# Another order of the seven products of w_co, with the sums made head by head and the second half's rows normalised first

## The chip, the cores and the metric

The kernel runs on one core of a Trainium2 chip. The metric is the device time of one execution in microseconds (us). The engines are TensorE (PE, with its weight loads as PEld), VectorE (DVE), ScalarE (ACT), GpSimd (POOL) and SyncE (SP), which issues the DMAs. Each engine works through its own queue in order.

## What is computed

One layer of an encoder trunk on x of 1024 tokens x 1024, in float32: a mixer (windowed attention and a gated DeltaNet), a cross-attention into 256 memory tokens, and a SwiGLU FFN. Each part is followed by an RMS norm, and its result is added to the residual stream. The change touches the cross-attention's output projection, what is around it, and the order of the rows from there on.

```python
def _memory_cross_attention(h, mem_n, w_q, w_kv, w_o):
    q = (h @ w_q).reshape(b, s, CROSS_HEADS, CROSS_HEAD_DIM)
    ...
    p = jax.nn.softmax(jnp.einsum('bqhd,bkhd->bhqk', q, k) * (CROSS_HEAD_DIM ** -0.5), axis=-1)
    o = jnp.einsum('bhqk,bkhd->bqhd', p, v).reshape(b, s, D_MODEL)
    return o @ w_o
...
    c = _memory_cross_attention(_rms_norm(x, g_cross_pre[l]), _rms_norm(mem, g_mem[l]), w_cq[l], w_ckv[l], w_co[l])
    x = x + _rms_norm(c, g_cross_post[l])
    f = _swiglu(_rms_norm(x, g_ffn_pre[l]), w_gate_up[l], w_down[l])
    x = x + _rms_norm(f, g_ffn_post[l])
```

## The kernel before

**Precision.** Every matmul operand is split into a high part (ACT casts it to fp32r, L103) and a low part (DVE or POOL subtracts the high part from the source, L104). A product takes three matmuls: high with high, high with low, low with high. `load_w` fetches weights over SP into `wraw` and splits them into `whi` and `wlo`.

**Stages.** The mixer comes first, then w_out by halves of 512 tokens (`mid_gemm`), then the cross-attention by halves (`cross_q`, `cross_attention`), w_co, the FFN's gate and up products, and w_down. Gate/up, w_co and w_down are computed with seven block products in place of eight: both operands are cut into 2 x 2 blocks, and sums of blocks take part in the products.

**Attention of a half.** For each of 4 heads: scores `pcs` (PE, L1158), maximum and its scaling `cmx` (DVE, L1160 and L1161), exponentials `cpr` (ACT, L1165), reciprocal `csum` and multiplication of `cpr` (DVE, L1167 and L1168), transposes `pct` (PE, L1174), their split into `cph` and `cpl`, and the value product `pco` (PE, L1184) of two column tiles ct = 2h and 2h + 1, each [128 columns x 512 tokens] and already transposed as w_co needs it.

**The blocks of the activations.** The first half's outputs are A11 (ct 0 to 3) and A12 (ct 4 to 7). They are copied to `raw` (`oraw`, L1188) and split in place into the query operand `q0`. The second half's are A21 and A22. For ct below 4 ACT copies A21 to `s1_` (tile `os1`, L1193), DVE subtracts it from A11 into `cs3` (L1195, a buffer of the tag `wpart`), and S3 = A11 - A21 is split into `q1`. For ct from 4 on A22 is split into `q1`, and DVE makes three sums in place: S1 = A21 + A22 in `s1_` (L1199), S2 = S1 - A11 in the first half of `raw` (L1200), S4 = A12 - S2 in its second half (L1201).

**The blocks of the weights.** w_co's four blocks b11, b12, b21, b22 are loaded over SP (8 transfers, tile `wco`) while the second half's attention runs, and POOL makes T1, T3, T2 and T4 from them in place by 16 differences (L1266; `sums` and `later`, called from the first two products).

**The seven products**, each 4 k tiles x 4 blocks of 128 tokens x 3 = 48 matmuls (L1245), in this order (names as in the prediction):

| | operands | banks | then |
|---|---|---|---|
| P1 | A11, B11 (both straight from `q0` and w_co) | A | ACT copies it to `e_` (L1319, tile `p1`) |
| P2 | A12, B21 | A, on top | ACT copies C11 to `c11` (L1323) |
| P3 | S3 (split in `q1`), T3 = `b12` | Y | DVE: `zv` = `e_` + Y |
| P4 | S2, T2 = `b22` | X | DVE: `e_` += X, `za` = `zv` + X |
| P5 | S1, T1 = `b11` | Z | DVE: `za` += Z |
| P6 | S4, B22 from w_co | Z, on top | DVE: `zz` high half = `e_` + Z |
| P7 | A22 (split in `q1`), T4 = `b21` | X, on top | DVE: `zv` += X |

P1 to P6 run k tile by k tile over all four token blocks (`block_product`); P7 runs block by block of tokens, so that its rows end one after the other. S2, S1 and S4 are split just before they are used, all three into one pair of tiles, `part` (`act_part`). Blocks of weights are split k tile by k tile into the tag `wpart` (`weight_part`, 7 buffers; a k tile takes two).

**The tail.** `zz` holds the first half's rows 0 to 3 (in blocks of 128 tokens), `zl` (`zv` and `za`) the rows 4 to 7. `square_of` (ACT, L1270) sums squares, `gained` (DVE or POOL, L1312) multiplies by the gain. `finish` takes one block of rows: it loads the residual `xr` over SP (L1279), makes the root on POOL (`prs`, L1281 and L1282), adds on DVE (L1283), stores x2 over SP (L1284), sums squares again on ACT (L1286), makes a second root on POOL (`pr`, L161 and L162) and normalises on ACT (L1290) or DVE (L1292). Rows 0 to 3 finish under P7 with the last step on ACT, rows 4 to 7 after it with the last step on DVE. Rows 0 and 1 have their own residual tile `xr01`, all others share two buffers `xr`. Then PE transposes the rows (`ptn`, L1367): the first four blocks of rows become X11 and X21, whose low parts POOL makes, and the last four go into X22 and the sums T1 to T4 of the FFN. The first FFN products (`pA`, L1412, EARLY = 4 pairs of gate and up) need the first four blocks of rows alone.

**Who sets the order.** The source gives the program order; a scheduler then places every instruction on its engine's queue by priority and by its own timeline. Weight loads and splits (`load_w`, `weight_part`, `act_part`) have a priority raised by AHEAD = 300, so they move ahead as far as their buffers allow.

Of the kernel before, what the change touches and what calls it, by code (L numbers as in the profile page):

```python
# [76 lines left out]
def tile_hybrid_block(  # L77
# [1057 lines left out]
    s1_ = rg.tile([P, KT // 2, HALF], F32, tag="os1", name="os1")  # L1135
# [10 lines left out]
    def cross_attention(q, hf):  # L1146
        for h in range(4):
# [31 lines left out]
            for j in range(2):  # L1179
# [11 lines left out]
                k = ct % (KT // 2)  # L1191
                if ct < KT // 2:
                    nc.scalar.copy(s1_[:, k], po)  # L1193
                    d_ = rg.tile([P, HALF], F32, tag="wpart", name="cs3", bufs=7)
                    nc.vector.tensor_tensor(d_, raw[:, k], po, ALU.subtract)  # L1195
                    split(q[0][:, k], q[1][:, k], d_)
                    continue
                split(q[0][:, ct, :], q[1][:, ct, :], po)
                nc.vector.tensor_tensor(s1_[:, k], s1_[:, k], po, ALU.add)  # L1199
                nc.vector.tensor_tensor(raw[:, k], s1_[:, k], raw[:, k], ALU.subtract)  # L1200
                nc.vector.tensor_tensor(raw[:, ct], raw[:, ct], raw[:, k], ALU.subtract)  # L1201
# [16 lines left out]
    zz = opC.tile([P, 4, D], F32, tag="x22", name="zz")  # L1218
# [3 lines left out]
    zl = tz.tile([P, 4, D], F32, name="zl")  # L1222
# [6 lines left out]
    def weight_part(b_, k):  # L1229
        with tc.high_priority(AHEAD):  # L1230
            dh, dl = (rg.tile([P, HALF], F32R, tag="wpart", name="wpart", bufs=7) for _ in range(2))
            split(dh, dl, b_[:, k])
        return dh, dl

    def act_part(a, k0):
        if isinstance(a, tuple):
            return [h[:, k0:k0 + 2] for h in a]
        with tc.high_priority(AHEAD):
            ah, al = (t[:, k0:k0 + 2] for t in part)
            split(ah, al, a[:, k0:k0 + 2])  # L1240
# [31 lines left out]
    def finish(r, z, eng):  # L1272

        tok = slice(r * P, (r + 1) * P)
        if r < 2:
            xr = xr01[:, r]
# [18 lines left out]
    s2_, s4_ = blocks(raw)  # L1295
# [28 lines left out]
    part = [p_.tile([P, HK, HALF], F32R, tag=t_, name="part") for p_, t_ in ((opB, b0 + "1"), (opB3, "b31"))]  # L1324
    Y = four([PG] * 4)
    block_product(Y, s3_, b12)
    for t in range(4):
        add(zv[:, t], e_[:, t], Y[t])
        square_of(c11[:, t], 0, t)
        gained(zz[:, t, LO], c11[:, t], LO)  # L1330
    X = four([PX] * 2 + [PN] * 2)
    block_product(X, s2_, b22, last=False)
    for t in range(4):
        add(e_[:, t], e_[:, t], X[t])
        add(za[:, t], zv[:, t], X[t])
    xr01 = opB3.tile([P, 2, D], F32, tag="b30", name="xr01")
    Z = four([PG] * 4)
    block_product(Z, s1_, b11, last=False)
    for t in range(4):
        add(za[:, t], za[:, t], Z[t])  # L1340
        square_of(za[:, t], 1, 4 + t)
        gained(za[:, t], za[:, t], HI)
    block_product(Z, s4_, (1, 1), first=False)
    for t in range(4):
        add(zz[:, t, HI], e_[:, t], Z[t])
        square_of(zz[:, t, HI], 1, t)
        gained(zz[:, t, HI], zz[:, t, HI], HI, nc.vector)
        finish(t, zz[:, t], nc.scalar)
    acts = [act_part(a22, k0) for k0 in (0, 2)]
    wts = [weight_part(b21, k) for k in range(HK)]  # L1350
    for t in range(4):
        for k in range(HK):
            ah, al = (h[:, k % 2] for h in acts[k // 2])
            three(X[t], ah, al, *wts[k], slice(t * P, (t + 1) * P), False, k == HK - 1, False)
        add(zv[:, t], zv[:, t], X[t])
        square_of(zv[:, t], 0, 4 + t)
        gained(zv[:, t], zv[:, t], LO, nc.vector)
        finish(4 + t, zl[:, t], nc.vector)
# [11 lines left out]
    def first_rows(j, k):  # L1370
        return zz[:, j, k * P:(k + 1) * P]

    def last_rows(j, k):
        return zl[:, j, k * P:(k + 1) * P]

    for k in range(KT):
        pt = turned_k(first_rows, k)
        nc.scalar.activation(raw[:, k, :], pt, AF.Identity, scale=gain("ffn", k))
        split(x1h[:, k, :], x1l[:, k, :], raw[:, k, :], eng=nc.gpsimd)
# [243 lines left out]

    def residual(t, after=None):
        xr = tp_.tile([P, D], F32, tag="xrf", name="xrf")
        with tc.issue_after((after or late).ins):
            nc.sync.dma_start(xr, d_x2[t * P:(t + 1) * P, :])
# [37 lines left out]
    def first_half(t):  # L1665
# [5 lines left out]
        nc.sync.dma_start(out[t * P:(t + 1) * P, :], z)  # L1671
# [14 lines left out]
    for t in range(4):  # L1686
# [20 lines left out]
        for z, o_ in ((za, 512), (zv, 0)):  # L1707
            nc.vector.scalar_tensor_tensor(z[:, t], z[:, t], rs, xr[:, o_:o_ + 512], ALU.mult, ALU.add)
            nc.sync.dma_start(out[r * P:(r + 1) * P, o_:o_ + 512], z[:, t])
# [32 lines left out]
```

## Time and profile before

| | us |
|---|---|
| median of 3 runs (lowest, highest) | 1556.82 (1551.7, 1563.44) |
| profiled execution, its time | 1557.34 |
| profiled execution, its span | 1555.6 |

The page of the profile covers one execution from its first to its last instruction (the span). Each row of instructions names the line, the engine, the operation and the tiles; in brackets at the end stands the idle time of the engine before it and what ended that. `pst` is the PSUM tile of all seven products. Mean granted PE clock over the span: 0.985 of full speed.

### The profile page before, as it was taken

Reading aid. Unit: us, or ns where it says so; the run is one execution under the profiler, and the core shown is the slowest. Engines: PE = TensorE matmul, PEld = TensorE weight load, DVE = VectorE, ACT = ScalarE, POOL = GpSimd, SP = SyncE. Lnnn points to the kernel's source line nnn. Section 1 sums busy time; section 2 is a strip of 40 time slices with the busy share of each in tenths; the row PEclk is TensorE's granted clock in tenths of the full one; section 3 lists DMA queues with packets and bytes.
Section 4 is the critical chain, followed back from the end, with each engine's and each line's share of the span. In section 5 each row is a group of like instructions: output and inputs, shape, how many; then the busy total and the mean of one; then the engine's idle time right before and its main releaser. Section 6 shows DMA issues by size and latency. Waiting matters only on the chain. (4 is left out here: it accounts for less than half of the span.)

```text
span 1555.6 us, 21081 instructions
## 1 busy us (share of the span) xinstructions
PE 1484.2 (95%) x7403; PEld 1243.1 (80%) x7403; DVE 1104.5 (71%) x1752; ACT 749.9 (48%) x1526; POOL 441.9 (28%) x436
## 2 busy tenths in 40 slices
PE   6999999998899899999998788999999999999998
PEld 5888888877899788888886567888888888888786
DVE  6868999776888865545388666776868554696665
ACT  6579722357567754545364564332323332454532
POOL 2020222302336103442251653433534333000021
PEclk9999999999999999999999799999999999999999
DMA  6244585847986764521422345344434333863355
GB/s 204 75 121 132 159 201 147 215 143 226 333 257 204 246 229 154 183 88 55 161 70 68 117 146 159 103 133 129 140 116 131 102 102 102 295 226 102 108 174 164
DMA packets 264167, 241.91 MB, mean 156 GB/s; under 512 B 33768, under 2 KB 203645, under 8 KB 264061
## 3 DMA queue, kind: packets, MB, share of 16 engines
q1 hardware_dynamic: 264061, 240.57, 49.5%
q8 instruction: 58, 0.95, 0.3%
q14 instruction: 48, 0.39, 0.1%
HBM read 171.02 MB, written 66.88 MB: 153 GB/s over the span
## 5 line engine op out<-in xcount | busy, mean ns | idle before, releaser
L103 ACT CAST whi<-wraw 128x1024 fp32r<-128x1024 f32 x98 | 103.1, 1053 | 156.2 <-issue 41.4
L104 POOL TENSOR_TENSOR wlo<-wraw,whi 128x1024 fp32r<-128x1024 f32 x38 | 91.8, 2415 | 184.3 <-ACT whi L103 182.8
L261 PE MATMUL pg<-hlo,whi 128*128 128x512 f32 x352 | 139.4, 396 | 0.0
L261 PE MATMUL pg<-hhi,whi 128*128 128x512 f32 x352 | 139.3, 396 | 0.0
L261 PE MATMUL pg<-hhi,wlo 128*128 128x512 f32 x352 | 138.5, 394 | 0.0
L1412 PE MATMUL pA<-b,whi 128*128 128x512 f32 x352 | 112.6, 398 | 6.5 <-POOL b L104 2.9
L104 DVE TENSOR_TENSOR wlo<-wraw,whi 128x1024 fp32r<-128x1024 f32 x60 | 79.2, 1322 | 46.7 <-ACT whi L103 44.1
L1412 PEld LDWEIGHTS pA<-b,whi 128*128 128x128 f32 x352 | 66.3, 191 | 22.2 <-POOL b L104 4.5
L1603 PE MATMUL pdX<-dhl,whi 128*128 128x512 f32 x264 | 76.1, 390 | 1.5 <-ACT dhl L103 0.8
L261 PEld LDWEIGHTS pg<-hhi,whi 128*128 128x128 f32 x352 | 66.4, 189 | 13.3 <-ACT hhi L103 0.2
L261 PEld LDWEIGHTS pg<-hhi,wlo 128*128 128x128 f32 x352 | 66.5, 189 | 12.8
L261 PEld LDWEIGHTS pg<-hlo,whi 128*128 128x128 f32 x352 | 66.3, 188 | 12.8
L1490 POOL TENSOR_TENSOR act<-act,up 128x512 f32<-128x512 f32 x33 | 49.8, 1509 | 91.5 <-DVE up L1489 60.5
L1412 PE MATMUL pA<-b,wlo 128*128 128x512 f32 x176 | 69.2, 395 | 0.2 <-DVE wlo L104 0.2
L103 ACT CAST whi<-araw 128x1024 fp32r<-128x1024 f32 (+1 forms) x36 | 35.4, 983 | 67.3 <-PE pdX L1603 24.5
L1633 POOL TENSOR_SCALAR frs<-sq 128x1 f32<-128x1 f32 x8 | 12.0, 1498 | 194.0 <-ACT jk L1622 193.1
L104 DVE TENSOR_TENSOR wlo<-araw,whi 128x1024 fp32r<-128x1024 f32 (+1 forms) x36 | 40.9, 1136 | 35.5 <-ACT whi L103 35.3
L286 DVE SCALAR_TENSOR_TENSOR acc<-cp,cols,acc 128x1024 f32<-128x1024 f32 x48 | 62.2, 1298 | 0.1
L1603 PEld LDWEIGHTS pdX<-dhl,whi 128*128 128x128 f32 x264 | 49.3, 188 | 12.8 <-ACT dhl L103 1.1
L1462 POOL TENSOR_TENSOR sr<-wraw 128x512 f32<-128x512 f32 x22 | 29.5, 1342 | 100.0 <-DMA wraw<-in_w_gate_up_dram 100.0
L1463 DVE TENSOR_TENSOR sr<-sr,wraw 128x512 f32<-128x512 f32 x22 | 36.7, 1667 | 28.1 <-POOL sr L1462 28.1
L1412 PE MATMUL pB<-s,s1h 128*128 128x512 f32 x176 | 54.3, 390 | 2.0 <-ACT s1h L103 2.0
(472 smaller groups left out, 4340.0 us busy)
## 6 DMA issues: line engine op xcount, KB each, us to landing
wraw<-in_w_gate_up_dram SPq DMA_DIRECT2D x52, 512.0 KB, 3.9
kv<-d_kv SPq DMA_DIRECT2D x32, 512.0 KB, 6.8
wraw<-in_w_in_dram SPq DMA_DIRECT2D x22, 512.0 KB, 4.6
b<-in_w_down_dram SPq DMA_DIRECT2D x20, 512.0 KB, 7.8
araw<-d_as SPq DMA_DIRECT2D x20, 512.0 KB, 3.7
pz<-d_pz SPq DMA_DIRECT2D x32, 256.0 KB, 6.6
wraw<-in_w_ckv_dram SPq DMA_DIRECT2D x16, 512.0 KB, 6.0
wraw<-in_w_out_dram SPq DMA_DIRECT2D x16, 512.0 KB, 3.7
```

Source lines behind the costliest of these rows:

```text
L103: nc.scalar.copy(hi, src)
L104: (eng or nc.vector).tensor_tensor(lo, src, f32(hi), ALU.subtract)
L261: nc.tensor.matmul(p_, w[:, k, :], ah[a][:, k, :], start=(k == 0 and i == 0), stop=(k == nk - 1 and i == 2))
L286: nc.vector.scalar_tensor_tensor(acc, cp[:, t:t + S], taps[t], acc, ALU.mult, ALU.add)
L1412: nc.tensor.matmul(out_, w[a][:, k, :], xx[b_][:, k, :], start=(start and k == 0 and i == 0), stop=(k == HK - 1 and i == 2), skip_group_ch ...
L1462: nc.gpsimd.tensor_tensor(s[0], b_[:, 0:HK], b_[:, HK:], ALU.add)
L1463: nc.vector.tensor_tensor(s[1], s[0], a_[:, 0:HK], ALU.subtract)
L1490: nc.gpsimd.tensor_tensor(o_, o_, up, ALU.mult)
L1603: nc.tensor.matmul(banks[t], a[:, k - k0, tt], w, start=(first and k == 0 and i == 0), stop=(k == NB - 1 and i == 2), skip_group_check=not ...
L1633: nc.gpsimd.tensor_scalar(rs, sq[:, 1, t:t + 1], sq[:, 0, t:t + 1], D * EPS, ALU.add, ALU.add)
```

## The change

The cross-attention's second half keeps no copy of A21. For ct from 4 on, S2 is made at once as (A22 - high part of S3) - low part of S3 (two DVE operations), split by ACT and DVE into `part` inside the attention's loop, and used to update `raw`: S1 = A11 + S2 in its first half, S4 = A12 - S2 in its second. The differences of the second half go into a tile `cs` of the attention's pool, and `wpart` has 9 buffers.

The order of the products becomes P1, P2, P3, P7, P4, P5, P6. P7 runs on top of P3 in the banks Y, after DVE has written P1 + P3 into `y7`, which is the memory of `b12`; so the sums after the products are four more operations. P4 takes S2 from `part`. The splits of S1 and S4 go into the memory of `q1` that P7 and P3 have read. P6 now runs by token blocks, with its weights loaded ahead from w_co.

Rows 4 to 7 are finished first, under P6, rows 0 to 3 after it, in both cases with the last step in turn on ACT and DVE. `zl` and `zz` change their pools, `xr45` takes the place of `xr01`. The FFN takes rows 4 to 7 as its first half; half of the low parts of X11 and X21 go to DVE. `there` puts the rows back when w_down reads the residual and stores the output.

```diff
--- before.py
+++ after.py
@@ -1132,7 +1132,6 @@
     raw = LR2.enter_context(pool("raw2", 1, side="right")).tile([P, KT, HALF], F32, name="oraw")
     LG = ExitStack()
     rg = LG.enter_context(pool("rg", 1, side="right"))
-    s1_ = rg.tile([P, KT // 2, HALF], F32, tag="os1", name="os1")
 
     def cross_q(hf):
         q = operand(opB, ("s1", "s2")[hf])
@@ -1188,17 +1187,26 @@
                     nc.scalar.copy(raw[:, ct], po)
                     split(q[0][:, ct, :], q[1][:, ct, :], po)
                     continue
-                k = ct % (KT // 2)
-                if ct < KT // 2:
-                    nc.scalar.copy(s1_[:, k], po)
-                    d_ = rg.tile([P, HALF], F32, tag="wpart", name="cs3", bufs=7)
+                k = ct % HK
+                if ct < HK:
+                    d_ = tx.tile([P, HALF], F32, tag="cs", name="cs")
                     nc.vector.tensor_tensor(d_, raw[:, k], po, ALU.subtract)
                     split(q[0][:, k], q[1][:, k], d_)
                     continue
                 split(q[0][:, ct, :], q[1][:, ct, :], po)
-                nc.vector.tensor_tensor(s1_[:, k], s1_[:, k], po, ALU.add)
-                nc.vector.tensor_tensor(raw[:, k], s1_[:, k], raw[:, k], ALU.subtract)
-                nc.vector.tensor_tensor(raw[:, ct], raw[:, ct], raw[:, k], ALU.subtract)
+                d_ = tx.tile([P, HALF], F32, tag="cs", name="cs")
+                nc.vector.tensor_tensor(d_, po, f32(q[0][:, k]), ALU.subtract)
+                nc.vector.tensor_tensor(d_, d_, f32(q[1][:, k]), ALU.subtract)
+                split(*(t[:, k] for t in s2_part()), d_)
+                nc.vector.tensor_tensor(raw[:, k], raw[:, k], d_, ALU.add)
+                nc.vector.tensor_tensor(raw[:, ct], raw[:, ct], d_, ALU.subtract)
+
+    part = []
+
+    def s2_part():
+        if not part:
+            part.extend(p_.tile([P, HK, HALF], F32R, tag=t_, name="part") for p_, t_ in ((opB, b0 + "1"), (opB3, "b31")))
+        return part
 
     q0 = cross_q(0)
     cross_attention(q0, 0)
@@ -1215,11 +1223,11 @@
 
 
     opC = LX.enter_context(pool("opC", 1))
-    zz = opC.tile([P, 4, D], F32, tag="x22", name="zz")
+    zl = opC.tile([P, 4, D], F32, tag="x22", name="zl")
     L3 = ExitStack()
     tz = L3.enter_context(pool("tz2", 1))
     gp = gpost_tile(tz, g_cross_post)
-    zl = tz.tile([P, 4, D], F32, name="zl")
+    zz = tz.tile([P, 4, D], F32, name="zz")
     zv, za = zl[:, :, 0:HALF], zl[:, :, HALF:]
     ssq = tz.tile([P, 2, NT], F32, name="ssq")
 
@@ -1228,13 +1236,14 @@
 
     def weight_part(b_, k):
         with tc.high_priority(AHEAD):
-            dh, dl = (rg.tile([P, HALF], F32R, tag="wpart", name="wpart", bufs=7) for _ in range(2))
+            dh, dl = (rg.tile([P, HALF], F32R, tag="wpart", name="wpart", bufs=9) for _ in range(2))
             split(dh, dl, b_[:, k])
         return dh, dl
 
     def act_part(a, k0):
         if isinstance(a, tuple):
             return [h[:, k0:k0 + 2] for h in a]
+        a, part = a
         with tc.high_priority(AHEAD):
             ah, al = (t[:, k0:k0 + 2] for t in part)
             split(ah, al, a[:, k0:k0 + 2])
@@ -1272,8 +1281,8 @@
     def finish(r, z, eng):
 
         tok = slice(r * P, (r + 1) * P)
-        if r < 2:
-            xr = xr01[:, r]
+        if 4 <= r < 6:
+            xr = xr45[:, r - 4]
         else:
             xr = tz.tile([P, D], F32, tag="xr", name="xr", bufs=2)
         nc.sync.dma_start(xr, d_x1[tok, :])
@@ -1292,7 +1301,7 @@
             nc.vector.tensor_scalar(z, xr, r2, None, ALU.mult)
 
     a11, a12, s3_, a22 = ((q_[0][:, c], q_[1][:, c]) for q_ in (q0, q1) for c in (slice(0, HK), slice(HK, KT)))
-    s2_, s4_ = blocks(raw)
+    s1_, s4_ = ([r_, [t[:, c] for t in q1]] for r_, c in zip(blocks(raw), (slice(HK, KT), slice(0, HK))))
 
     def four(spec):
         return [p_.tile([P, HALF], F32, tag=t_, name="pst") for p_, t_ in spec]
@@ -1321,41 +1330,41 @@
     c11 = opB3.tile([P, HK, HALF], F32, tag="b30", name="c11")
     for t in range(4):
         nc.scalar.copy(c11[:, t], A[t])
-    part = [p_.tile([P, HK, HALF], F32R, tag=t_, name="part") for p_, t_ in ((opB, b0 + "1"), (opB3, "b31"))]
     Y = four([PG] * 4)
-    block_product(Y, s3_, b12)
+    block_product(Y, s3_, b12, last=False)
+    y7 = b12
     for t in range(4):
-        add(zv[:, t], e_[:, t], Y[t])
+        add(y7[:, t], e_[:, t], Y[t])
+    block_product(Y, a22, b21, first=False)
+    for t in range(4):
         square_of(c11[:, t], 0, t)
         gained(zz[:, t, LO], c11[:, t], LO)
+        add(zv[:, t], e_[:, t], Y[t])
     X = four([PX] * 2 + [PN] * 2)
-    block_product(X, s2_, b22, last=False)
+    block_product(X, tuple(part), b22)
     for t in range(4):
+        add(zv[:, t], zv[:, t], X[t])
+        square_of(zv[:, t], 0, 4 + t)
+        gained(zv[:, t], zv[:, t], LO)
+        add(za[:, t], y7[:, t], X[t])
         add(e_[:, t], e_[:, t], X[t])
-        add(za[:, t], zv[:, t], X[t])
-    xr01 = opB3.tile([P, 2, D], F32, tag="b30", name="xr01")
+    xr45 = opB3.tile([P, 2, D], F32, tag="b30", name="xr45")
     Z = four([PG] * 4)
     block_product(Z, s1_, b11, last=False)
     for t in range(4):
         add(za[:, t], za[:, t], Z[t])
         square_of(za[:, t], 1, 4 + t)
-        gained(za[:, t], za[:, t], HI)
-    block_product(Z, s4_, (1, 1), first=False)
+        gained(za[:, t], za[:, t], HI, nc.vector)
+        finish(4 + t, zl[:, t], (nc.scalar, nc.vector)[t % 2])
+    acts = [act_part(s4_, k) for k in (0, 2)]
+    wts = [load_w(w_co[(HK + k) * P:(HK + k + 2) * P, HI], 2, HALF) for k in (0, 2)]
     for t in range(4):
+        for k in range(HK):
+            three(Z[t], *(h[:, k % 2] for h in (*acts[k // 2], *wts[k // 2])), slice(t * P, (t + 1) * P), False, k == HK - 1, False)
         add(zz[:, t, HI], e_[:, t], Z[t])
         square_of(zz[:, t, HI], 1, t)
         gained(zz[:, t, HI], zz[:, t, HI], HI, nc.vector)
-        finish(t, zz[:, t], nc.scalar)
-    acts = [act_part(a22, k0) for k0 in (0, 2)]
-    wts = [weight_part(b21, k) for k in range(HK)]
-    for t in range(4):
-        for k in range(HK):
-            ah, al = (h[:, k % 2] for h in acts[k // 2])
-            three(X[t], ah, al, *wts[k], slice(t * P, (t + 1) * P), False, k == HK - 1, False)
-        add(zv[:, t], zv[:, t], X[t])
-        square_of(zv[:, t], 0, 4 + t)
-        gained(zv[:, t], zv[:, t], LO, nc.vector)
-        finish(4 + t, zl[:, t], nc.vector)
+        finish(t, zz[:, t], (nc.scalar, nc.vector)[t % 2])
     LG.close()
 
     x1h, x1l = operand(opB, "s1")
@@ -1368,15 +1377,15 @@
         return pt
 
     def first_rows(j, k):
+        return zl[:, j, k * P:(k + 1) * P]
+
+    def last_rows(j, k):
         return zz[:, j, k * P:(k + 1) * P]
-
-    def last_rows(j, k):
-        return zl[:, j, k * P:(k + 1) * P]
 
     for k in range(KT):
         pt = turned_k(first_rows, k)
         nc.scalar.activation(raw[:, k, :], pt, AF.Identity, scale=gain("ffn", k))
-        split(x1h[:, k, :], x1l[:, k, :], raw[:, k, :], eng=nc.gpsimd)
+        split(x1h[:, k, :], x1l[:, k, :], raw[:, k, :], eng=(nc.gpsimd, nc.vector)[k % 2])
     tr = LR2.enter_context(pool("tr", 1, side="right"))
     T2, T4 = (blocks(t) for t in operand(opA, "s0"))
     T1, T3 = (blocks(t) for t in operand(opB, "s2"))
@@ -1621,10 +1630,14 @@
         jk = tp_.tile([P, 512], F32, tag="jk", name="jk", bufs=1)
         nc.scalar.activation(jk, src, AF.Square, accum_out=sq[:, ch, t:t + 1])
 
+    def there(t):
+        r = (t + NT // 2) % NT
+        return slice(r * P, (r + 1) * P)
+
     def residual(t, after=None):
         xr = tp_.tile([P, D], F32, tag="xrf", name="xrf")
         with tc.issue_after((after or late).ins):
-            nc.sync.dma_start(xr, d_x2[t * P:(t + 1) * P, :])
+            nc.sync.dma_start(xr, d_x2[there(t), :])
         return xr
 
     def rstd_at(t):
@@ -1668,7 +1681,7 @@
         z = zz[:, t]
         nc.vector.tensor_tensor(z[:, 512:], z[:, 512:], gp[:, 512:], ALU.mult)
         nc.vector.scalar_tensor_tensor(z, z, rs, xr, ALU.mult, ALU.add)
-        nc.sync.dma_start(out[t * P:(t + 1) * P, :], z)
+        nc.sync.dma_start(out[there(t), :], z)
 
     t4h = keep.tile(BLOCK, F32R, tag="b22", name="t4h")
     t4l = kz.tile(BLOCK, F32R, tag="b11", name="t4l")
@@ -1706,7 +1719,7 @@
         rs = rstd_at(r)
         for z, o_ in ((za, 512), (zv, 0)):
             nc.vector.scalar_tensor_tensor(z[:, t], z[:, t], rs, xr[:, o_:o_ + 512], ALU.mult, ALU.add)
-            nc.sync.dma_start(out[r * P:(r + 1) * P, o_:o_ + 512], z[:, t])
+            nc.sync.dma_start(out[there(r), o_:o_ + 512], z[:, t])
     LB.close()
     L0.close()
```

## The prediction

> **What bounds the kernel now.** I read the page first, then the busy time by stretches, then who TensorE (PE) waits for, then the instructions in order of time.
>
> ```profile
> span 1555.6 us, 21081 instructions
> ...
> PE 1484.2 (95%) x7403; PEld 1243.1 (80%) x7403; DVE 1104.5 (71%) x1752; ACT 749.9 (48%) x1526; POOL 441.9 (28%) x436
> ```
>
> PE is busy for 95% of the span, so time can only be won where PE has gaps or a low clock. The change touches the stage from about 776 to 960 us (attention of the second half, the seven products of w_co, the norms, the first FFN products). In the next rows the columns are the stretch, its length, the busy time of each engine and, after POOL, the granted clock.
>
> ```profile
> 776.00:799.00 23.00, 22.58 (x132) 19.73 (x131) 22.14 (x30) 12.99 (x35) 22.96 (x15) 1.00 0.31 103
> 799.00:821.00 22.00, 22.00 (x106) 18.16 (x105) 17.93 (x30) 14.55 (x27) 0.00 (x0) 1.00 0.16 48
> 821.00:840.00 19.00, 13.24 (x54) 9.31 (x52) 15.15 (x18) 9.25 (x17) 6.81 (x4) 1.00 0.28 88
> 840.00:880.00 40.00, 37.35 (x152) 29.77 (x152) 30.27 (x38) 14.52 (x28) 15.78 (x14) 0.93 0.24 83
> 880.00:920.00 40.00, 24.58 (x102) 16.98 (x103) 23.32 (x25) 31.68 (x54) 25.05 (x31) 0.80 0.41 149
> 920.00:960.00 40.00, 36.06 (x161) 28.89 (x160) 26.12 (x36) 22.09 (x37) 14.27 (x10) 0.97 0.49 155
> ```
>
> PE idles 5.8 us in 821 to 840, 2.7 in 840 to 880, 15.4 in 880 to 920, 3.9 after, and its clock is below 1 from 840 on. In 776 to 799 PE is full, but so are VectorE (DVE, 22.1 of 23) and GpSimd (POOL, 23.0 of 23). PE's waits in 785 to 960 us, as total, number and longest:
>
> ```profile
> PE ptn L1367 <- ACT zz L1290: 6.2, 3, 2.8
> PE pst L1245 <- DVE wpart L104: 3.6, 2, 2.3
> PE pA L1412 <- POOL b L104: 2.9, 4, 1.1
> PE pst L1245 <- DVE os L1199: 2.5, 2, 1.9
> ...
> PE pst L1245 <- DVE part L104: 1.0, 1, 1.0
> PE pst L1245 <- ACT part L103: 1.0, 1, 1.0
> ...
> PE pco L1184 <- DVE cpl L104: 0.4, 1, 0.4
> ```
>
> The pst rows are the w_co products: 3.6 + 2.5 + 1.0 + 1.0 = 8.1 us of waits on the sums of the second half's heads and on split weights. The ptn and pA rows are the tail: normalised rows and their splits.
>
> **The change, part by part.** I call the products P1 (A11), P2 (A12), P3 (S3), P4 (S2), P5 (S1), P6 (S4), P7 (A22). Before they run in this order; after it is P1 P2 P3 P7 P4 P5 P6. All stay at 48 matmuls, so PE's work does not change.
>
> *P7 moved up, behind the last head.* PE's own rows:
>
> ```profile
> 812.77 5.39 PE L1245 MATMUL pst<-wpart,b 128*128 128x512 f32 x23
> 820.95 2.88 PE L1245 MATMUL pst<-wpart,part 128*128 128x512 f32 x12
> ...
> 839.91 11.00 PE L1245 MATMUL pst<-wpart,part 128*128 128x512 f32 x40 [1.03 <-DVE part L104]
> 870.01 4.47 PE L1245 MATMUL pst<-wpart,b 128*128 128x512 f32 x19
> 876.83 2.87 PE L1245 MATMUL pst<-wpart,b 128*128 128x512 f32 x8 [2.35 <-DVE wpart L104]
> ```
>
> A matmul costs (5.39 - 0.39) / 22 = 0.227 us at full clock (0.39 is its latency). P3 ends at 820.95 and the last product at 876.83 + 2.87 = 879.7: 58.7 us for four products and the last head's 12 value matmuls, 204 x 0.227 = 46.3. So 12.4 us are lost: 8.1 in the waits, 1.8 in the row at 839.91 (11.00 against 40 x 0.227 + 0.16 = 9.2), the rest in smaller slow stretches. In the new order P7 stands where P4 waited. It needs no sum, only A22 and weights, and lasts 48 x 0.227 = 10.9 us. Under it DVE makes the last two S2 blocks: two low parts, two times two subtractions, four updates of raw, two low parts of S2, 12 operations of 0.69 us (row at 801.49 below) = 8.3 us. That fits, by 2.6 us. P4, P5 and P6 find their operands split into memory that P3 and P7 have left, so the waits of ACT and DVE on "part" go too. The weights get 9 buffers for 7, 4.5 parts ahead for 3.5, and the last product's weights come whole from w_co, so the 2.35 us at 876.83 go. I count the whole 12.4 us as won here, and charge below what comes back. DVE's added work (S2 by its own operations, four more sums, four splits taken from POOL in the tail: some 8 us net) and ACT's saved copies cost or save nothing here: DVE has 3.9 + 9.7 us free in 821 to 880, and PE does not wait for ACT there.
>
> *Four splits moved into the busiest stretch.* With 9 buffers and no cs3 in them, the four splits of P3's weights come earlier: in the built order DVE does them among the softmax of heads 1 and 2, where before they came from 801 us on.
>
> ```profile
> 774.11 24.86 POOL L1266 TENSOR_TENSOR wco<-wco 128x512 f32<-128x512 f32 x16 [20.93 <-DMA wco<-in_w_co_dram]
> ```
>
> ```profile
> 781.59 1.59 DVE L1168 TENSOR_TENSOR cpr<-cpr,csum 128x512 f32<-128x512 f32 x1
> ...
> 786.17 1.67 DVE L104 TENSOR_TENSOR b<-cs,b 128x512 fp32r<-128x512 f32 x1
> ...
> 788.93 0.68 DVE L104 TENSOR_TENSOR b<-cs,b 128x512 fp32r<-128x512 f32 x1
> ...
> 790.13 0.68 DVE L104 TENSOR_TENSOR cpl<-pct,cph 128x512 fp32r<-128x512 f32 x1
> ...
> 801.49 0.69 DVE L104 TENSOR_TENSOR wpart<-wco,wpart 128x512 fp32r<-128x512 f32 x1
> ```
>
> ```profile
> 784.14 2.43 PE L1158 MATMUL pcs<-kr,b 128*128 128x256 f32 x19
> 786.41 0.60 PE L1174 MATMUL pct<-ident,cpr 128*128 128x128 f32 x4
> ```
>
> While POOL makes its 16 differences, a DVE operation of this size on SBUF alone takes 1.59 or 1.67 us, or 0.68 when it meets none; from 801 us, with POOL quiet, 0.69. So the four cost 2.8 to 6.7 us, and 5.2 at the mean of the three rows (1.31), with what stands behind them: the multiplication of the probabilities and then cpl, which PE's pco needs. cpl ended at 790.8; after, a reduction (0.7) moves behind it and the splits ahead: 792.9 to 796.8, 795.3 at the mean. PE reaches that pco at 784.1 + 24 x 0.12 (scores) + 0.7 to 1.2 (8 transposes) + 19 x 0.227 = 792. So it waits 0.9 to 4.8 us, 3.3 at the mean; 0.4 of that was there before. Cost 0.5 to 4.4, and I take 3, since the rows beside POOL are the nearest. The granted clock then dips as it did before 840: 5.8 us idle cost 1.8, so 3 us cost 0.9 (0 to 1.8).
>
> The Trainium skill ("SBUF — State Buffer", section "SBUF: two separate sides") says that a DVE operation with two SBUF inputs and a GpSimd operation exclude each other for a whole instruction. By that each split could wait out a whole difference and the sum would end near 1552 us; the rows agree that they exclude each other but show at most 1.67 us, so the rows stand. The Trainium skill ("TensorE: Matmul & The Clock Gate", section "Part 1: The HAM clock gate") also says that PE falls to half clock after an idle window of about 3.4 us and needs about as long to come back. By that a wait of 3 us costs nothing, or 1.7 us if it fills a window; the slow row at 839.91 came after waits of at most 1.9 us in one piece, so here the trace has the clock fall sooner than the rule.
>
> *The second half's rows first.* The tail keeps its form: a product ends, four rows are normalised under the next product (P6 by row blocks, 10.9 us, where P7 was), then transposed.
>
> ```profile
> L1283 DVE SCALAR_TENSOR_TENSOR xr<-zz,prs,xr x4: 1274/1277/1279, 872.0 to 878.5; 128x1024 f32<-128x1024 f32 x4
> L1286 ACT ACTIVATE zz<-xr x4: 1041/1042/1066, 873.3 to 885.4; 128x1024 f32<-128x1024 f32 x4
> ...
> L1290 ACT ACTIVATE zz<-xr,pr x4: 1135/1142/1149, 880.2 to 888.8; 128x1024 f32<-128x1024 f32 x4
> ...
> L1292 DVE TENSOR_SCALAR zl<-xr,pr x4: 752/1248/1750, 899.8 to 910.9; 128x1024 f32<-128x1024 f32 x4
> ...
> DMA to landing us min/median/max: 2.6/3.0/4.2
> ```
>
> ```profile
> 901.19 6.42 POOL L104 TENSOR_TENSOR b<-oraw,b 128x512 fp32r<-128x512 f32 x4
> ```
>
> Before, the product ended at 870.0 and the fourth row was ready at 888.8 + 1.1 = 889.9, 19.9 us later. Now two of the four last steps go to DVE (0.75 to 1.75 for ACT's 1.14), which takes up to 2.3 us off ACT's queue; but two weight casts stand in that queue between them, so the gain is 0 to 1.5. Every other split of the transposed rows goes from POOL (6.42 / 4 = 1.6) to DVE (0.69), against PE's 2.9 us of waits on "POOL b": 0 to 2.9. Together 0 to 4.4; I take 1.5, since DVE's normalisations of the other rows now stand ahead of these splits. The swapped output rows, the reversed stores and the residual reads in w_down move no bytes more and no operation: nothing. SP issues the same loads; only two w_gate_up loads move behind row stores and xr loads, and ACT's first casts use loads that are in long before: nothing.
>
> Sum: 12.4 - 3 - 0.9 + 1.5 = 10.0 us. Against the profiled execution's 1557.34 us (span 1555.6 and 1.7 around it), which stands 0.5 above the median of 1556.82, that gives 1547 us. After this stage the built order is the same on every engine and PE is the bound, so the 10 us reach the end.
>
> **The rivals.** *More than that.* The splits meet POOL's gaps, the tail's gains come whole, and the clock recovers: in 880 to 920 it lost 24.58 x 0.20 = 4.9 us; half of it back is 2.4. 12.4 - 0.5 + 4.4 + 2.4 = 18.7 us: 1539. For it: all waits on sums go, and short stalls go with the clock. Against: the tail is still a chain through ACT, POOL and DVE.
>
> *The wait is replaced.* Each split waits for a whole difference, 24.86 / 16 = 1.55 us: 4 x (0.69 + 1.55) = 9.0 us, cpl at 790.8 - 0.7 + 9.0 = 799.1, PE stalls 7.1, 6.7 more than before, and the clock takes 1.8. Besides, P7's matmuls now wait until DVE has read P3's sums out of the same four banks, 4 x 0.69 = 2.8 us behind DVE's other work. 12.4 - 6.7 - 1.8 - 2.8 + 1.5 = 2.6: 1555. This is where the Trainium skill's exclusion ("SBUF — State Buffer", same section) would lead in full. For it: DVE had only 0.9 us free in 776 to 799. Against: at 788.93 a split passed in 0.68.
>
> *Slower.* The first rows come late in the tail. Two buffers serve the residual loads of the last four rows, so each pair waits until the pair before it is normalised, and in PE's queue two transposes of the last rows stand ahead of 14 early FFN matmuls. One round is a load (3.0 to 4.2), 1.28, 1.04, POOL's root and 1.14, some 8 to 9 us, and there are two. If ACT, which now squares these rows between the casts, holds a normalisation back by 8 us in both, 16 us come on PE: 12.4 - 3.9 - 16 = -7.5: 1565. It decides from 8.5 us of added delay. For it: ACT is busy 31.7 of 40 in 880 to 920. Against: ACT loses steps there, and the early products give PE work.
>
> **How the numbers follow.** The likeliest case has 0.55, with its own range 1541 (12.4 - 0.5 + 4.4 = 16.3) to 1551 (12.4 - 4.4 - 1.8 = 6.2). More than that 0.17, the replaced wait 0.17, slower 0.11. The range 1538 to 1557 leaves out the slower case and the far tail of the first rival. A difference of 1% (15.6 us) is about what a measurement of this kernel can tell from none. Faster by over 1% needs less than 1541.2: nearly all of the first rival and a little of the likeliest, 0.20. Slower by over 1% needs more than 1572.4: half of the slower case, 0.05. Within 1%: 0.75.
>
> **What would show it.** Right: no pst wait on os, part or wpart after the last head; the last product ends about 8 to 9 us earlier than 879.7; a wait of PE's pco on cpl of some 3 us between 786 and 800; DVE's wpart operations of over 1.2 us there. Wrong: no such wait (the first rival), one of over 6 us or pst waiting for the sums of P3 (the second), or the transposes of the last rows waiting longer than 2 us each (the third).

## The result, and the profile after

The kernel after takes 1540.2 us (median of 4 runs, 1537.9 to 1542.8), the kernel before 1557.6 us (4 runs on the same chip, 1551.7 to 1563.4). The ratio is 0.989, with a 95% interval of 0.985 to 0.993. The profiled execution took 1542.75 us against 1557.34, 14.6 less; the rest of this section reads that one. It is the slowest of the kernel after's four executions, so the gains read from it may be somewhat low.

The page of the kernel after:

```profile
span 1541.0 us, 21093 instructions
...
PE 1479.5 (96%) x7403; PEld 1242.7 (81%) x7403; DVE 1106.6 (72%) x1766; ACT 746.9 (48%) x1524; POOL 436.5 (28%) x432
```

Its busy time in the stretches shown of before (stretch, length, PE, PEld, DVE, ACT, POOL, granted clock, DMA share, GB/s):

```profile
776.00:799.00 23.00, 18.33 (x89) 15.75 (x88) 20.87 (x25) 11.91 (x27) 23.00 (x15) 0.85 0.20 71
799.00:821.00 22.00, 22.00 (x115) 18.64 (x114) 17.57 (x31) 11.96 (x28) 0.04 (x1) 1.00 0.21 62
821.00:840.00 19.00, 19.00 (x87) 15.64 (x85) 19.00 (x31) 10.62 (x17) 0.00 (x0) 1.00 0.30 96
840.00:880.00 40.00, 34.37 (x152) 27.80 (x150) 31.99 (x45) 21.84 (x46) 27.88 (x27) 0.97 0.21 81
880.00:920.00 40.00, 36.30 (x159) 28.03 (x160) 27.14 (x33) 32.55 (x56) 18.50 (x20) 0.86 0.61 209
920.00:960.00 40.00, 35.57 (x159) 28.25 (x158) 27.86 (x37) 18.76 (x31) 16.95 (x12) 1.00 0.50 152
```

A new hole of 4.7 us, with a clock of 0.85, stands in 776 to 799; the hole of 821 to 840 is gone; 880 to 920 lost 15.4 us before and loses 3.7 now. PE's waits from 770 to 946 us (total, number, longest):

```profile
PE ptn L1376 <- ACT zl L1299: 5.8, 2, 5.3
PE pct L1173 <- DVE cs L1193: 3.9, 1, 3.9
PE pB L1421 <- ACT s1h L103: 2.0, 1, 2.0
PE pA L1421 <- POOL b L104: 1.8, 1, 1.8
...
PE pcs L1157 <- ACT cpr L1164: 0.8, 1, 0.8
```

No wait of pst, the w_co products, is left, and one of pct is new. PE's rows give the milestones:

```profile
821.43 5.74 PE L1254 MATMUL pst<-wpart,b 128*128 128x512 f32 x24
827.00 0.40 PE L1183 MATMUL pco<-cph,vr 128*128 128x512 f32 x1
...
873.11 0.39 PE L1254 MATMUL pst<-whi,b 128*128 128x512 f32 x1
...
943.73 0.73 PE L1421 MATMUL pB<-s,s1h 128*128 128x512 f32 x2 [2.03 <-ACT s1h L103]
```

P3 ends at 827.0, the last product at 873.11 + 0.39 = 873.5, and pB, the first FFN product that needs the last rows, starts at 943.7 (958.5 before). I count from the start of the cross-attention's first projection (pcq). The code ahead of it is the same in all kernels here, and yet it starts at 641.5 to 647.0 us in their profiles, so distances compare better than times:

| us | before | after |
|---|---|---|
| pcq starts at | 646.7 | 646.0 |
| pcq to the end of P3 ("attention") | 174.3 | 181.0 |
| end of P3 to the last product ("products") | 58.7 | 46.5 |
| last product to pB ("tail") | 78.8 | 70.2 |
| pcq to pB | 311.8 | 297.7 |

So the attention lost 6.7 us, the products won 12.2 and the tail 8.6: 14.1 in all. From pB to the end nothing moved (597.1 and 597.3 us).

### The profile page after: what moved, and what is told of

Its sections match the earlier page's. It is cut to its first block, busy times and chain, and to the rows that moved or that the text cites. A ratio compares the mean times of both kernels' runs of the same rounds, so it can differ in the third digit from the quotient of the medians.

```text
span 1541.0 us, 21093 instructions
## 1 busy us (share of the span) xinstructions
PE 1479.5 (96%) x7403; PEld 1242.7 (81%) x7403; DVE 1106.6 (72%) x1766; ACT 746.9 (48%) x1524; POOL 436.5 (28%) x432
## 4 chain that ended last, share of the span: by engine, by line
PE 69%; DVE 10%; DMA 8%; ACT 5%; issue 3%; POOL 2%; SPq 2%; DVEq 0%; POOLq 0%; ACTq 0%
PE pD L1421 8%; PE pE L1421 8%; PE pA L1421 7%; PE pcq L261 6%; PE pmg L1068 6%; PE pdX L1612 6%; PE pg L261 5%; PE pB L1421 4%; PE pst L1254 4%; PE psc L809 3%; PE pdA L1612 2%; PE pdX L1709 2%; PE pdD L1612 2%; DVE acc L286 2%; PE pco L1183 1%
```

## The experiments

### Where the attention lost 6.7 us

DVE's rows of the kernel after, where the loss begins:

```profile
776.17 0.68 DVE L104 TENSOR_TENSOR cpl<-pct,cph 128x512 fp32r<-128x512 f32 x1
778.92 1.12 DVE L104 TENSOR_TENSOR wpart<-wco,wpart 128x512 fp32r<-128x512 f32 x1 [2.06 <-ACT wpart L103]
779.97 1.25 DVE L1160 TENSOR_SCALAR cmx<-cmx 128x2 f32<-128x2 f32 x1
...
784.69 1.76 DVE L104 TENSOR_TENSOR wpart<-wco,wpart 128x512 fp32r<-128x512 f32 x1
786.38 1.75 DVE L1167 TENSOR_TENSOR cpr<-cpr,csum 128x512 f32<-128x512 f32 x1
...
788.23 1.56 DVE L1167 TENSOR_TENSOR cpr<-cpr,csum 128x512 f32<-128x512 f32 x1
789.72 0.68 DVE L1193 TENSOR_TENSOR cs<-oraw,pco 128x512 f32<-128x512 f32 x1
790.31 1.16 DVE L104 TENSOR_TENSOR wpart<-wco,wpart 128x512 fp32r<-128x512 f32 x1
...
793.09 1.77 DVE L104 TENSOR_TENSOR wpart<-wco,wpart 128x512 fp32r<-128x512 f32 x1
```

And PE's:

```profile
785.81 0.74 PE L1157 MATMUL pcs<-kr,b 128*128 128x256 f32 x4 [0.78 <-ACT cpr L1164]
790.45 1.12 PE L1173 MATMUL pct<-ident,cpr 128*128 128x128 f32 x4 [3.89 <-DVE cs L1193]
...
794.77 0.63 PE L1254 MATMUL pst<-wlo,b 128*128 128x512 f32 x1
...
795.73 0.39 PE L1254 MATMUL pst<-wlo,b 128*128 128x512 f32 x1
```

pct starts when cs ends (789.72 + 0.68 = 790.40). cs reads the value product of head 0 out of a PSUM bank; the pool `pn` has two banks for pct and pco, so head 1's pct needs the one that cs empties. It also needs head 1's multiplied probabilities, and the second multiplication ends only at 788.23 + 1.56 = 789.79: the bank is the last of two late things, by 0.6 us. When PE goes on, it runs at half rate (four transposes in 1.12 us for 0.60, a matmul in 0.63 for 0.39) until about 795.4, 4.9 us, of which half is lost: 2.4. The waits come to 3.9 + 0.8, less 0.4 that was there before. Together 6.7.

**The splits behind head 1's softmax, then behind head 2's.** In both, `weight_part` is given an order beside its priority; the mark is head 1's last split of pct (first kernel) or head 2's second multiplication (second kernel).

```
     def weight_part(b_, k):
-        with tc.high_priority(AHEAD):
+        with ExitStack() as order_:
+            order_.enter_context(tc.high_priority(AHEAD))
+            if b_ is b12:
+                order_.enter_context(tc.issue_after(mark))
```

> The kernel after, but the four weight splits of P3 are issued on ACT and DVE only behind head 1's last split of the turned probabilities (about 799 us), when GpSimd has made its 16 differences; nothing else is moved by hand. Theory one: the attention lost 6.8 us (P3 ends at 827.0 for 820.95, from a first projection 0.7 us earlier) because these four splits stood in DVE's queue ahead of the softmax's multiplication while GpSimd was at work. Then PE's wait at pct on the probabilities (3.9 us) goes, P3 ends at 820.5 to 822, and the time falls by 5 to 6.5 us against the kernel after, to about 1534.5. Theory two: the attention lost the time to the order of PE's queue or to the second half's other work, not to the splits. Then P3 ends at 826 to 827.5 and the time stays within 1.5 us of 1540. Theory three: the splits are then late for P3 itself, and PE waits for wpart between 799 and 812 instead; P3 ends at 823 to 826.

1541.8 us (ratio to before 0.990, 0.988 to 0.992), attention 180.2 us: PE waits 3.7 us at head 2's pct instead of head 1's.

> The kernel after, but the four weight splits of P3 are issued behind head 2's second multiplication of the probabilities (about 798 us), the last softmax step that is made beside GpSimd's differences; in the first trial they stood ahead of it, and the wait at pct came one head later. Theory one (DVE against GpSimd, and what stands behind it in DVE's queue): no split of P3 meets a difference, each takes about 0.69 us, PE's waits at pct and pcs come to less than 1.5 us in all, P3 ends at 820.5 to 822.5, 174.5 to 176 us behind the first projection (181.0 in the kernel after, 174.25 in the kernel before), and the time falls to 1533 to 1537. Theory two (the loss is not the splits'): P3 ends 179.5 us or more behind the first projection, and the time stays at 1539 to 1542. Theory three (the splits are now late): PE waits for wpart between 805 and 815, and P3 ends 177 to 179.5 us behind it.

1540.9 us (0.990, 0.989 to 0.991), attention 179.0. DVE's and PE's rows of this second kernel:

```profile
794.74 1.60 DVE L1169 TENSOR_TENSOR cpr<-cpr,csum 128x512 f32<-128x512 f32 x1
796.26 4.65 DVE L104 TENSOR_TENSOR wpart<-wco,wpart 128x512 fp32r<-128x512 f32 x4
800.83 1.27 DVE L1195 TENSOR_TENSOR cs<-oraw,pco 128x512 f32<-128x512 f32 x2
```

```profile
801.55 0.66 PE L1175 MATMUL pct<-ident,cpr 128*128 128x128 f32 x4 [3.66 <-DVE cs L1195]
```

By the numbers theory two fits both, but the rows say something else: the splits now stand straight ahead of head 1's cs, and pct waits for that. I had moved them past the multiplication, which ended at 796.34, and not past the operation that PE waited for. So here the bank alone holds PE.

**The splits behind head 1's second cs.** The same edit with that mark, `marks[3]`.

> The kernel after, but the four weight splits of P3 are issued behind the second subtraction cs of head 1. Two trials moved PE's wait at pct by one head without ending it: each time it ended 0.05 us after the first cs, the subtraction that reads the head's value product out of a PSUM bank. There are two such banks, and pct needs the one that cs empties. New theory: what costs is that cs stands in DVE's queue behind the splits, whatever it is that slows these. Then PE waits less than 0.8 us at pct, P3 ends 174.3 to 176 us behind the first projection (181.0 after, 174.25 before), and the tail being as after, the time is 1533.5 to 1537. If DVE's load among GpSimd's differences is the cause and not the place of cs, the wait moves once more, to head 3: P3 ends 178 us or more behind it, and the time is 1539 to 1542.

1535.2 us (0.986, 0.984 to 0.987), attention 173.4, products 46.7, tail 70.6. No wait of pct or pcs is left:

```profile
795.23 1.27 DVE L1195 TENSOR_TENSOR cs<-oraw,pco 128x512 f32<-128x512 f32 x2
796.43 1.85 DVE L104 TENSOR_TENSOR wpart<-wco,wpart 128x512 fp32r<-128x512 f32 x1
798.80 0.68 DVE L104 TENSOR_TENSOR wpart<-wco,wpart 128x512 fp32r<-128x512 f32 x1
```

```profile
776.00:799.00 23.00, 23.00 (x135) 20.17 (x135) 22.38 (x29) 13.51 (x33) 21.72 (x14) 1.00 0.24 83
```

So the whole loss came from the place of these four splits: in the kernel after two of them stand ahead of head 0's cs, in the two trials above all four ahead of head 1's. Of the kernels that make all the sums, none found is clearly faster than this one; its interval lies below those of the two trials above. The kernel after's own interval (0.985 to 0.993) is too wide to part the two by times alone; from pcq to pB it is 290.7 us for 297.7.

**Early splits, but GpSimd's differences cut to 8 columns.**

```
-        nc.gpsimd.tensor_tensor(o_, a, b_, ALU.subtract)
+        nc.gpsimd.tensor_tensor(o_[:, 0:8], a[:, 0:8], b_[:, 0:8], ALU.subtract)
```

> The kernel after, but GpSimd's 16 differences of w_co's blocks are made on 8 of 512 columns, so most of the weights' sums are left out; the four early splits stay where the scheduler puts them, among the softmax of heads 0 and 1. If the loss in the attention is DVE against GpSimd (theory one), each wpart split falls from 1.1 to 1.8 us to about 0.69, the multiplications of the probabilities from 1.6 to 1.75 to below 1.2, PE does not wait over 1 us at pct, and P3 ends at 820 to 822 us. If the four splits cost their place in the queue by themselves, without GpSimd (theory two), P3 still ends at 824 to 827. After this stage nothing is removed, so the span is 1534 to 1537 by the first and 1538 to 1541 by the second.

One run, 1532.1 us, attention 173.5. Two splits take 1.30 us together, the multiplications 0.69, and PE waits nowhere from 776 to 840:

```profile
770.86 1.30 DVE L104 TENSOR_TENSOR wpart<-wco,wpart 128x512 fp32r<-128x512 f32 x2 [3.86 <-ACT wpart L103]
...
787.42 0.69 DVE L1167 TENSOR_TENSOR cpr<-cpr,csum 128x512 f32<-128x512 f32 x1
```

So splits ahead of cs cost nothing when GpSimd is hardly at work. The place is not quite the same, though: here the scheduler put all four between 770.86 and 775.23, at most 132.6 us behind the start of pcq, where the kernel after has its first at 132.9 (778.92), and GpSimd's results were there sooner. The run removes the slower operations and the wait for GpSimd together and does not part them.

**Early splits, and ACT empties the bank.**

```
-                    nc.vector.tensor_tensor(d_, raw[:, k], po, ALU.subtract)
+                    nc.scalar.copy(d_, po)
+                    nc.vector.tensor_tensor(d_, raw[:, k], d_, ALU.subtract)
```

> The kernel after with its early splits where they are, but for heads 0 and 1 ACT copies the value product out of its PSUM bank into the tile of cs, and DVE subtracts from that copy in SBUF (four copies more, the same results). If pct waits for the bank, PE's wait at pct goes though DVE is as late as before: below 1 us for 3.9, and P3 ends 175 to 177.5 us behind the first projection instead of 181.0; the subtractions then meet GpSimd's differences and take 1.2 to 1.8 us for 0.68. If pct waits for the probabilities themselves, whose multiplication stands between the same splits, the wait stays at 2 to 4 us and P3 ends 179 us or more behind it.

1541.3 us (0.990, 0.988 to 0.992), attention 181.7: nothing won. PE's waits have other names, 5.4 us in all:

```profile
PE pct L1173 <- ACT wpart L103: 1.7, 1, 1.7
PE pcs L1157 <- ACT cpr L1164: 1.6, 1, 1.6
...
PE pct L1173 <- DVE cpr L1167: 1.2, 1, 1.2
...
PE pco L1183 <- DVE csum L1166: 0.9, 1, 0.9
```

```profile
785.95 1.76 DVE L1194 TENSOR_TENSOR cs<-oraw,cs 128x512 f32<-128x512 f32 x1
```

My expectation missed: the bank was only the last of the late things. With it freed, PE meets the same delay at the softmax's steps (the first wait bears the name of ACT's cast, but a multiplication that pct needs ended within 0.1 us of it), and cs from SBUF takes 1.76 us for 0.68.

### What covers the products

**P4 ahead of P7.** The two `block_product` calls change places, with the additions to match.

```
-    block_product(Y, a22, b21, first=False)
     X = four([PX] * 2 + [PN] * 2)
     block_product(X, tuple(part), b22)
+    block_product(Y, a22, b21, first=False)
```

> The kernel after, but P4, the product with the second sum, comes straight behind P3 and P7 behind it; the sums of the last head go to their own memory as in the kernel after, and the products are added up in another order that gives the same rows. If P7's place is what hides DVE's work on the last head's sums (8.3 us of it), PE waits again for the sums' parts behind the last head, 2.5 to 5.5 us, and from the end of P3 to the last product go 49.5 to 53 us instead of 46.5, and the time is 1543 to 1547. If the gain came from the memory of their own for the split sums and from the two more weight buffers alone, those waits stay below 1 us, the stretch at 46.5 to 47.5 us and the time at 1539.5 to 1541.5.

1539.1 us (0.990, 0.988 to 0.992), attention 179.0, products 47.9, tail 66.9. One small wait is new, on a sum that DVE reads out of a bank:

```profile
PE pst L1254 <- DVE zl L1318: 1.1, 1, 1.1
```

No wait on the last head's sums comes back. But the scheduler itself puts 16 matmuls of P7, 16 x 0.227 = 3.6 us, between those of P4. So P7's place by hand is worth 1.4 us of the 12.2, not the 3 to 6.5 expected; what the stretch would cost without any of P7 under the sums, this run does not show.

**Both moves together:** late splits (behind cs) and P4 first.

> Both moves that helped or should help: P3's four splits behind head 1's second cs, and P4 ahead of P7. From the end of P3 to pB the order with P4 first took 114.8 us for 116.7. If the two gains stand by themselves, P3 ends 174.3 to 176 us behind the first projection, pB comes 289 to 291 us behind it (297.7 in the kernel after, 311.8 before), and the time is 1531 to 1535. If the first order's gain came from GpSimd's earlier start in that run, pB comes 291 to 293 us behind it and the time is that of the kernel with late splits alone.

1535.0 us (0.986, 0.984 to 0.988), attention 174.6, products 48.7, tail 67.9, pcq to pB 291.3 (290.7 with late splits alone). The order of P4 and P7 makes no difference that these runs can tell.

**Seven buffers for nine,** in the kernel with splits behind cs: `bufs=9` becomes `bufs=7`.

> The kernel with the four splits of P3 behind head 1's second cs (the best so far, 1535.2 us), but with 7 buffers for split weights in place of 9, as the kernel before had. Between the end of P3 and the last product it took 46.7 us with 9 (58.7 in the kernel before, 46.3 at full clock). If the two added buffers carry part of the cover, as the wait of 2.3 us on a split weight in the kernel before suggests, PE waits for wpart again, 1 to 3.5 us, and the stretch takes 48 to 50.5 us, the time 1536.5 to 1539. If the memory of the sums' splits alone carries it, no wait on wpart comes back and the stretch stays at 46.5 to 47.5, the time at 1534 to 1536.5.

1535.5 us (0.988, 0.986 to 0.989), products 47.7 for 46.7. Two waits of 0.3 us on split weights are back:

```profile
PE pst L1259 <- DVE wpart L104: 0.6, 2, 0.3
```

The two buffers are worth 1.0 us in the profile, less than expected of them, and nothing that the times can tell.

### Where the tail won 8.6 us

**Low parts of the turned rows all on GpSimd.** `eng=(nc.gpsimd, nc.vector)[k % 2]` becomes `eng=nc.gpsimd`.

> The kernel after, but all eight low parts of the first rows' turned blocks are made on GpSimd again, as before, in place of four on DVE. The tail from the last w_co product to the first pB matmul took 78.8 us before and 70.2 after. If the alternation of these low parts brought the gain, the waits of pA on GpSimd's parts come back (2.9 us before, 1.8 after) and the tail takes 73 to 76 us, the time 1543 to 1546. If the gain came from elsewhere (the alternate last step, or the order of the rows), the tail takes 70 to 72 us and the time is 1540 to 1542.

1540.9 us (0.990, 0.988 to 0.992), tail 69.9: this alternation brings nothing here.

**The last step as before,** `nc.scalar` for the first group's rows and `nc.vector` for the second's.

> The kernel after, but the last step of the normalisation is on ACT for all four rows of the first group and on DVE for all four of the second, as before, in place of alternating. If this alternation brought the tail's gain, the first transposes come 1 to 2.5 us later (the row at 880.3 moves to 881.5 to 883), the wait of ptn on ACT grows from 5.3 to 6.5 us or more, and the tail takes 72 to 76 us for 70.2, the time 1542 to 1546. If it did not, the tail takes 70 to 71.5 us and the time is 1540 to 1541.5.

1546.6 us (0.994, 0.992 to 0.996), tail 75.6, 5.4 us longer. PE waits for the rows and, later, for ACT's copies of pA:

```profile
PE ptn L1376 <- ACT zl L1299: 7.3, 4, 4.1
PE pA L1421 <- ACT m L1438: 4.8, 2, 3.5
```

**The kernel before with the two alternations, then with the last step's alone.**

```
-        finish(t, zz[:, t], nc.scalar)
+        finish(t, zz[:, t], (nc.scalar, nc.vector)[t % 2])
...
-        finish(4 + t, zl[:, t], nc.vector)
+        finish(4 + t, zl[:, t], (nc.scalar, nc.vector)[t % 2])
...
-        split(..., eng=nc.gpsimd)
+        split(..., eng=(nc.gpsimd, nc.vector)[k % 2])
```

> The kernel before, with one part of the change alone: in the tail the last step of the normalisation alternates between ACT and DVE in both groups of rows, and the low parts of the first turned rows alternate between GpSimd and DVE. Attention and products stay as before (last product at about 879.7). Undone in the kernel after, these two cost 5.4 us (the last step) and nothing (the low parts). If they are worth the same here, the tail from the last product to the first pB falls from 78.8 to 73 to 74.5 us, the time by 4 to 6 us, to about 1551.5, and the other 3 us of the tail's gain are the new order of rows. If they are worth it only with the second half's rows first, the tail stays at 77.5 to 79 us and the time within 1.5 us of the kernel before.

1544.8 us (0.993, 0.991 to 0.994), tail 68.5: 10.3 us less than before and 1.7 less than in the kernel after. Both forecasts were too high.

> The kernel before, with only the alternation of the normalisation's last step between ACT and DVE; the low parts of the turned rows stay on GpSimd. With both alternations the tail from the last product to pB took 68.5 us for 78.8. If the last step is all of it, as in the kernel after, where the low parts were worth nothing, the tail takes 67.5 to 70 us and the time is 1543.5 to 1547. If the low parts are worth the 2.9 us that pA waits for GpSimd's parts in the kernel before, the tail takes 70.5 to 73 us and the time is 1546.5 to 1549.

1547.7 us (0.996, 0.994 to 0.998), tail 71.0. The last step's alternation alone wins 7.8 us. The low parts' 2.5 us on top are less sure: in the nine kernels here that share the kernel after's code of the tail, it took 66.9 to 70.8 us. For the second half's rows first no gain in the tail can be told: with the low parts on GpSimd it took 69.9 us with this order and 71.0 without, with the low parts in turn 70.2 and 68.5.

## Why the prediction was right, and where it was not

The total was near (1547 forecast, 1540.2 measured, in the range), but by two errors of opposite sign: in the profile 14.1 us came out of this stage where the sum had 10.0. That it came so near is luck in part. The likeliest case had its own range, 1541 to 1551, and the result lies just outside it, beside the first rival's 1539 and below the 1541.2 to which I gave 0.20. That rival's reasons came only by half: the tail's gains came whole, but the splits did not all meet GpSimd's gaps.

**The cover of the waits, 12.4 us: right in size** (12.2, no pst wait left), **its reason shown only in part.** I let P7's place carry it. P4 first costs 1.4 us, but with 3.6 us of P7 still among P4's matmuls; seven buffers cost 1.0. What remains lies with what no run undid: a P7 that can run while the sums are made, sums split head by head into memory of their own, and the last product's weights taken whole from w_co. Which of these does how much stays open.

**The four moved splits, 3 us, and the clock, 0.9: too small.** They cost 6.7 together. The step that failed put only the splits' own time ahead of cpl, and let PE meet it at pco. The rows show three things that it missed. DVE stood idle for 2.06 us at the first split, whose high part ACT could only make when GpSimd's third difference was done (ACT's cast starts at 778.26): a raised priority put a waiting operation at the head of the queue. The small operations between grew too (cmx 1.25 us, for 0.45 and 0.62 in the same steps before). And PE met the delay earlier, at the bank that cs empties, at 789.72; DVE's row of the kernel before has it 4.9 us earlier:

```profile
784.81 1.27 DVE L1195 TENSOR_TENSOR cs<-oraw,pco 128x512 f32<-128x512 f32 x2
```

The clock took 2.4 us, not 0.9. The rival of the replaced wait was nearer in size: 6.7 + 1.8 = 8.5 for the 6.7 measured, where I had 3.9. Its other half, P7 waiting for P3's sums, did not come.

**The tail, 1.5 us: too small by far.** It won 8.6. The step that failed took the alternation as 2.3 us off ACT's queue in the first group of rows, less two casts, and gave the second group nothing. The first group's rows in the kernel after:

```profile
L1299 ACT ACTIVATE zl<-xr,pr x2: 1146/1148/1150, 872.8 to 879.1; 128x1024 f32<-128x1024 f32 x2
L1299 ACT ACTIVATE zz<-xr,pr x2: 1148/1156/1164, 887.7 to 898.1; 128x1024 f32<-128x1024 f32 x2
...
L1301 DVE TENSOR_SCALAR zl<-xr,pr x2: 753/754/754, 873.7 to 878.0; 128x1024 f32<-128x1024 f32 x2
L1301 DVE TENSOR_SCALAR zz<-xr,pr x2: 746/746/746, 891.0 to 901.5; 128x1024 f32<-128x1024 f32 x2
```

The first group's fourth row is ready at 879.1 + 1.15 = 880.2, 17.6 us after its product (862.6), for 19.9 before: 2.3, the size that I had and then cut. The second group's is ready at 901.5 + 0.75 = 902.2, 28.7 us after the last product, for 910.9 + 1.75 - 879.7 = 33.0 before: 4.3 more that I had left out, though PE's transposes waited only 1.5 us for these rows before. In all PE idles 12.67 us between the last product and pB, for 19.64 before, which is 7.0 of the 8.6; the granted clock there went from 0.88 to 0.90. The slower rival's transposes of the last rows did not wait at all.

**The signs I had named:** no pst wait: so. The last product 8 to 9 us earlier: 6.2. pco waiting for cpl: no, pct for cs. Splits over 1.2 us: 1.12, 1.76, 1.16 and 1.77.

## What to carry to other kernels

Before an operation is let forward in a queue by priority, ask what it waits for itself, and what stands behind it: a wait at the head of an in-order queue holds up everything behind it, as the 2.06 us did here. It need not cost: in the run with the short differences DVE idled 3.86 us at its first split, and PE did not wait. When a wait has a name, ask what the named operation frees (here a PSUM bank) and who else reads the same engine's results, since freeing the one only shows the next. And where rows are finished one by one, an engine's share in the last step can be worth more (5.4 and 7.8 us here) than the order of two products.

## What the runs showed of the hardware

**DVE beside GpSimd.** Operations of 128x512 with both inputs in SBUF took 1.56 to 1.85 us where they met a difference in full, about 1.1 or 0.68 where they fell into a gap, and 0.68 with GpSimd quiet. With one input in PSUM they keep 0.68 beside it (789.72 above). The same subtraction took 0.68 from PSUM and 1.76 from a copy in SBUF. The Trainium skill ("SBUF — State Buffer", section "SBUF: two separate sides") names this pair, two SBUF inputs against a GpSimd operation that reads SBUF, among those that exclude each other; the trace agrees. A difference lasts about 24.61 / 16 = 1.54 us here, and the wait on top of 0.68 stayed at 1.17 or less. That 128x2 operations go to 1.25 us as well I had not expected; why, no run shows.

```profile
774.43 24.61 POOL L1275 TENSOR_TENSOR wco<-wco 128x512 f32<-128x512 f32 x16 [21.94 <-PE pct L1173]
```

**The clock.** Six waits of nearly the same length, each at a pct for cs, had different prices. The granted clock stood at half for 3.4 or 6.8 us in one piece, and what counts is how much of that fell on PE's work:

| kernel | wait, us | half clock from, to | of it PE at work | wait and half of that work |
|---|---|---|---|---|
| the kernel after | 3.89 | 788.5, 795.4 | 4.9 | 6.3 |
| low parts all on GpSimd | 3.89 | 788.2, 795.0 | 4.1 | 5.9 |
| the last step as before | 3.90 | 790.1, 796.9 | 5.7 | 6.8 |
| P4 ahead of P7 | 3.92 | 785.0, 788.4 | 2.8 | 5.3 |
| splits behind head 1's softmax | 3.70 | 800.4, 807.2 | 5.9 | 6.7 |
| splits behind head 2's | 3.66 | 802.9, 806.3 | 3.4 | 5.4 |

The first three have the same code up to there. So such a wait cost 1.4 to 1.8 times its length. Of the 2.0 us by which the attention was shorter with P4 first (179.0 for 181.0), 1.0 is this, and 0.8 a wait of pcs that did not come. Three stretches of the kernel after, then two of the kernel whose bank ACT empties (the granted clock stands after POOL):

```profile
785.80:788.40 2.60, 0.74 (x4) 0.54 (x4) 2.57 (x4) 0.62 (x1) 2.60 (x3) 1.00 0.24 93
788.40:790.40 2.00, 0.00 (x0) 0.00 (x0) 2.00 (x3) 0.00 (x0) 2.00 (x2) 0.53 0.00 0
790.40:795.30 4.90, 4.85 (x20) 4.57 (x21) 4.90 (x5) 4.12 (x8) 4.90 (x4) 0.50 0.00 0
...
781.00:784.30 3.30, 0.49 (x3) 0.20 (x2) 3.27 (x4) 2.74 (x7) 3.30 (x3) 1.00 0.04 17
784.30:787.70 3.40, 3.30 (x15) 3.30 (x16) 3.40 (x4) 0.42 (x1) 3.40 (x3) 0.50 0.00 0
```

The Trainium skill ("TensorE: Matmul & The Clock Gate", section "Part 1: The HAM clock gate") gives an idle window of about 3.4 us and as long a way back. The lengths at half clock fit that. The idle window does not, taken as one unbroken wait: the clock fell 2.0 us into the wait of 3.89 us, and in the second kernel it fell after waits of 1.73 us and 1.18 us with transposes between them.
